# ScalarE and VectorE in program order through the feed-forward layers, their borders by token half, and products of a split grouped by engine

## The chip, the cores and the metric

One core of a Trainium2 chip runs the whole program. The metric is the device time of one execution in microseconds (us). A core has five engines that run their own queues in order: TensorE (PE, matrix products and transposes; PEld is its weight load), VectorE (DVE), ScalarE (ACT), GpSimd (POOL) and SyncE (SP), which here only issues transfers.

## The reference, cut to what matters

256 tokens of width 1024 pass through two stacked blocks in fp32. What the change touches are the five SwiGLU layers (width 2816) and what stands between them:

```python
def swiglu(h, w_gu, w_down):
    gu = h @ w_gu
    return (jax.nn.silu(gu[..., :D_FF]) * gu[..., D_FF:]) @ w_down
...
        x = x + rms_norm(y, g[1])
        y = memory_cross_attention(rms_norm(x, g[2]), mem_n, wq[i], wkv[i], wo[i])
        x = x + rms_norm(y, g[3])
        y = swiglu(rms_norm(x, g[4]), w_gu[i], w_down[i])
        x = x + rms_norm(y, g[5])
...
    for i in range(DEPTH_2):
        x = x + 0.5 * swiglu_2(rms_norm_2(x, ffn1_norm[i]), ffn1_w_gate[i], ffn1_w_up[i], ffn1_w_down[i])
        h = rms_norm_2(x, mix_norm[i])
        # i = 0: attention (8 heads, rotary, causal); i = 1: Mamba-2 (32 heads in 8 groups)
        x = x + 0.5 * swiglu_2(rms_norm_2(x, ffn2_norm[i]), ffn2_w_gate[i], ffn2_w_up[i], ffn2_w_down[i])
```

The first block normalizes each sublayer's output before it adds it to x (the gains g[1], g[3], g[5]); the second adds it as it is.

## The kernel before

Every weight comes in units of 128 x 2048 fp32 (1 MB). A unit is split into a high part, rounded to the matmul's fp32r type, and a low part, the rest. `unit` (L185) loads it into one of three raw buffers (SP), and for each of its two 1024-column halves ACT rounds it (L198 or L205, "cast") and DVE subtracts (L199 or L207, "rest"); for some units POOL subtracts. A product is then three matmuls: high by high, low by high, high by low (`mm`, L181). Activations are split likewise (`split`, L299). Cast halves live in four buffers each for high and low (`pw`); an "ahead" unit has two whole 1 MB tiles from a pool of seven that the normed input and x share (`p8`). There are four PSUM banks for passing use (`psb`) and four for sums (`psa`).

The order of PE's work is the order of the program (`manual_schedule` with PE alone, L930 and L937). The order of ACT's, DVE's, POOL's and SP's queues is chosen at build time by a scheduler that takes what is ready by its own estimate, earliest in the program first; `high_priority` moves instructions forward in that choice. `weave` (L463) interleaves PE's filling work (products with weights, a step at a time) with latency chains (heads, groups) that are due at given steps and name the steps until their next piece.

A feed-forward layer (`ffn`, L1079) has 11 chunks of 256 hidden columns. A chunk multiplies both token halves (128 tokens each) by two units of gate and up weights (`wide_step`, eight steps of six 512-column matmuls), evicts Silu(gate)*up (`evict`, L1094 on ACT, L1095 on DVE), and turns and splits the chunk before (`turned`, L1101, L301, L303) so that `down_steps` (L275) can multiply that by its down unit and add it up in the four sum banks. Chunks 0 and 10 go by token half. The last down unit alone goes by token half too, and after each quarter `Fin.done` (L410) updates x: where the output is normalized first, Square of the sums with a row sum (L426, ACT), the root (L430, L317 on DVE, L318 on POOL), scaling and adding (L436, L437, DVE) of both column halves; else one addition (L414). Then come the squares of x for the next norm (`PreT.square`, L370, ACT) and the turning of x into the next layer's input (`PreT.turn`: four transposes L378 on PE, then four scalings L383 on ACT and four rests L384 on DVE, in turn by column block). Where the output is normalized, all four turns are put off until after the last unit ("late"): two run before the next layer's first matmul and two after its steps 1 and 3.

The borders are: from the mixing stage to the memory attention (normalized, at 262 us of the profile; the last value unit `mem_v_unit` stands between, with two turns at its step 3 and two behind it), from there to the first layer (normalized, 333 us), to the second (normalized, 525 us), to the attention (720 us), back (840 us), to the fourth layer (1025 us), to the Mamba stage (1212 us), and to the last layer (1465 us).

The attention's chain of a head pair is `pair` (L1209): `rope_norm` (L1170), E0 = 5 steps, the turning of q and k (L1201), scores, E2 = 6 steps, the turning of the weights. `rope_tables` (L1027) are made behind the memory attention. The Mamba stage's chain is `group` (L1421): a convolution (L1402 DVE, L1405 ACT, taps L131 DVE), two pairs of heads whose decay sums PE multiplies out (two matmuls of `ahl` by `ohr`) and ACT evicts by four Relus (L1440), the two masked products of a head pair (L1452, DVE), D0 = 2 steps, the gate and turning, D1 = 5 steps, the output products (three banks), squares and root (L1496 to L1499), the root's product with a row scale (L1500, DVE), the scaling (L1502, ACT), D2 = 9 steps, and the turning of y. Every `wz` unit's rest is POOL's (L207 on POOL).

Of the kernel before, what the change touches and what calls it, by code (L numbers as in the profile page):

```python
# [97 lines left out]
def _build(ctx, nc, tc, a):  # L98
# [112 lines left out]

    def lin_step(bk, u, xh, xl, k, m, last=7):
# [7 lines left out]
    def lin_pair(bks, us, xh, xl, k, last=7):  # L220

        for lo_ in (False, True):
# [32 lines left out]
    def wide_step(bks, us, xh, xl, k, halves=(0, 1)):  # L255

        h, l = us[k // 4]
# [9 lines left out]
    def down_part(acc, u, hh, hl, th, o, k, first, last):  # L267
        t, c = slice(th * 128, th * 128 + 128), slice(o * 512, o * 512 + 512)
        h, l = u[0][k][:, c], u[1][k][:, c]
# [5 lines left out]
    def down_steps(acc, u, yf, first, fin=None, every=2):  # L275

        hh, hl = yf()
        if fin is not None:
            for th in range(2):
                for o in range(2):  # L280
                    for k in range(2):
                        down_part(acc, u, hh, hl, th, o, k, first, True)
                    fin.done(th, o)
                    yield
            return
# [77 lines left out]
    class PreT:  # L363
# [8 lines left out]
        def turn(self, xt, th, q):  # L372
# [8 lines left out]
            for i in range(4):  # L381
                k, b = 4 * q + i, bk[:, i * 128:i * 128 + 128]
                S.mul(self.xh[:, k, t], b, pc(gname, gi + k))  # L383
                V.scalar_tensor_tensor(self.xl[:, k, t], b, pc(gname, gi + k), f(self.xh[:, k, t]), MUL, SUB)  # L384
# [7 lines left out]
    class Fin:  # L392
# [10 lines left out]
        def turn(self, th, q):  # L403
            self.nxt.turn(self.xt, th, q)

        def turns(self, *w):
            for th, q in w:
                self.late.append(lambda th=th, q=q: self.turn(th, q))

        def done(self, th, o):  # L410
            xt, c = self.xt, slice(o * 512, o * 512 + 512)
            x, y = xt[:, th, c], flat(self.acc[2 * th + o])
            if self.post is None:
                V.tensor_tensor(x, x, y, ADD)  # L414
                if self.nxt is None:
                    nc.sync.dma_start(a["out"][:, th, c], x)
                    return
                self.nxt.square(th, o, x)
                if th:
                    self.turn(0, o)  # L420
                    self.turns((1, o))
# [9 lines left out]
            r = rstd(v, 1.0 / 1024, 1e-6, n=1)  # L431
            for o in range(2):
# [5 lines left out]
                self.nxt.square(th, o, x)  # L438
            self.turns((th, 0), (th, 1))
# [461 lines left out]
    def mem_v_unit(j, u, pool, late):  # L901
        mh_, ml_, rbm, rm = kv["x"]
        bk = bank(pool)
        for k in range(8):
            linT_step(bk, u, mh_, ml_, k)
            if k == 3:
                late.pop(0)()
# [6 lines left out]
    def wout_units():  # L914
        acc.extend([bank(psa), bank(psa), bank(psa), bank(psf)])
        for j, y in enumerate([y_r[0], *y_c]):
            hl = split(y)
            yield from down_steps(acc, unit(a["wout"][(2, 0, 1)[j]]), lambda: hl, j == 0, None, 1)
# [19 lines left out]
    order.__enter__()  # L938
    yl = split(y_r[1])
    u = unit(a["wout"][3])  # L940
# [4 lines left out]
    run(down_steps(acc, u, lambda: yl, False, fin))  # L945
    mem_v_unit(3, um, psb, fin.late)
    for t in fin.late:
        t()
# [3 lines left out]
    def two(n, l):  # L952
        return lambda: (unit(a[n][l * 22], True, ahead=True), unit(a[n][l * 22 + 1]))
# [54 lines left out]
    acc, nf = [], []  # L1008
    nxt2 = PreT("g4")
    fins = []  # L1010

    def outs_():
        acc.extend(new_acc())
        for h in range(4):
            u = unit(a["wo"][h], True)
            if h == 3:
                nf.extend(two("wgu", 0)())
                fins.append(Fin(xt, acc, nxt2, "g3r"))
            yield from down_steps(acc, u, lambda: oh[h], h == 0, fins[0] if h == 3 else None)

    fill = [first_heads()]
    for h in (2, 3):
        fill.append(pieces(lambda h=h: unit(a["wq"][h], True), qb[h]))
    fill.append(outs_())
    weave(fill, [(8, mem_head(0)), (9, mem_head(1)), (11, mem_head(2)), (15, mem_head(3))])

# [607 lines left out]
```

## Time and profile before

| what | value |
|---|---|
| median of the runs shown (3 runs) | 1662.89 us (1662.61 to 1665.56) |
| the profiled execution | 1663.16 us, span 1661.1 us |
| PE busy | 1600.0 us (96%) |
| DVE, ACT, POOL busy | 1058.9 (64%), 864.0 (52%), 142.9 us (9%) |
| mean granted TensorE clock | 0.987 |
| HBM read | 263.52 MB, 159 GB/s over the span |

The span runs from the first to the last instruction; 2.1 us lie around it. A matmul's shown length overlaps that of the next, so the rate is read from stretches, not from single lengths. The clock column of a stretch is the mean of the two levels that were granted, 1.00 (2.4 GHz) and 0.50 (1.2 GHz).

### The profile page before, as it was taken

The numbers are of one execution on the slowest core, as the hardware profiler recorded it, in microseconds if no ns is written. First come the engines' busy times: TensorE is split into PE (matmuls) and PEld (weight loads), VectorE is DVE, ScalarE is ACT, GpSimd is POOL, SyncE is SP. The second block draws the span as 40 slices with busy tenths as digits, with TensorE's granted clock in tenths as the row PEclk, the third lists the DMA queues.
The fourth block names the chain that finished last, engine by engine and source line by source line (L and its number), as shares of the span: only waits on it lengthen the run. The fifth ranks groups of instructions, "written<-read, shape, count | busy, mean of one in ns | idle before, by whom it ended". The sixth has DMA issues, their size and how long they took to land.

```text
span 1661.1 us, 21983 instructions
## 1 busy us (share of the span) xinstructions
PE 1600.0 (96%) x8702; PEld 1376.1 (83%) x8702; DVE 1058.9 (64%) x1652; ACT 864.0 (52%) x1432; POOL 142.9 (9%) x154
## 2 busy tenths in 40 slices
PE   8999998989999999999999999999999999999999
PEld 7898988878887888877778887888889889778887
DVE  6888855574545554567665556555559999665453
ACT  6734445563445444456664445444456766564442
POOL 2322200000000000000000000000014333000000
PEclk9999999989999999999999999999999999999999
DMA  7321234445454445452345554554533323455451
GB/s 280 133 76 53 88 131 149 150 147 213 165 217 157 159 181 200 172 193 92 140 191 200 179 193 175 188 201 170 195 121 129 151 102 127 150 206 194 186 188 66
DMA packets 39848, 265.99 MB, mean 160 GB/s; under 512 B 4673, under 2 KB 5441, under 8 KB 8385
## 3 DMA queue, kind: packets, MB, share of 16 engines
q1 hardware_dynamic: 39456, 263.41, 43.0%
q8 instruction: 68, 1.11, 0.3%
q10 hardware_dynamic: 288, 1.18, 0.2%
q14 instruction: 36, 0.29, 0.1%
HBM read 263.52 MB, written 1.05 MB: 159 GB/s over the span
## 4 chain that ended last, share of the span: by engine, by line
PE 77%; DVE 13%; ACT 6%; issue 3%; POOL 1%; DMA 0%; SPq 0%; POOLq 0%; ACTq 0%; DVEq 0%
PE bk L181 74%; DVE wl L207 3%; PE bk L1101 1%; ACT wh L205 1%; DVE s2w L1427 1%; DVE cv L131 1%; DVE s2w L131 1%; DVE sm L1500 1%; ACT s2w L1405 1%; ACT s2w L1440 1%; PE bk L740 1%; ACT s2n L370 0%; PE bk L378 0%; ACT s L383 0%; DVE s2w L436 0%
## 5 line engine op out<-in xcount | busy, mean ns | idle before, releaser
L181 PE MATMUL bk<-wh,s 128*128 128x512 f32 (+1 forms) x2400 | 735.6, 381 | 10.2 <-DVE s L384 4.8
L207 DVE TENSOR_TENSOR wl<-raw,wh 128x1024 fp32r<-128x1024 f32 x344 | 420.2, 1227 | 266.0 <-ACT wh L205 264.3
L205 ACT CAST wh<-raw 128x1024 fp32r<-128x1024 f32 x366 | 382.0, 1049 | 291.2 <-PE bk L181 278.9
L181 PEld LDWEIGHTS bk<-wh,s 128*128 128x128 f32 x2400 | 441.3, 190 | 94.4 <-DVE s L384 8.2
L181 PE MATMUL bk<-wl,s 128*128 128x512 f32 (+1 forms) x1200 | 449.8, 375 | 0.0
L181 PE MATMUL bk<-wh,s2f 128*128 128x512 f32 x1072 | 344.6, 392 | 0.0
L181 PEld LDWEIGHTS bk<-wl,s 128*128 128x128 f32 x1200 | 228.0, 190 | 37.0
L181 PEld LDWEIGHTS bk<-wh,s2f 128*128 128x128 f32 x1072 | 201.3, 188 | 41.6 <-issue 0.2
L181 PE MATMUL bk<-s,wh 128*128 128x256 f32 x1120 | 220.2, 296 | 8.7 <-ACT wh L528 5.9
L181 PE MATMUL bk<-wl,s2f 128*128 128x512 f32 x536 | 208.6, 389 | 0.0
L181 PEld LDWEIGHTS bk<-s,wh 128*128 128x128 f32 x1120 | 180.7, 197 | 12.8 <-ACT wh L528 5.9
L199 DVE TENSOR_TENSOR wl<-raw,wh 128x1024 fp32r<-128x1024 f32 x120 | 144.4, 1221 | 66.1 <-ACT wh L198 66.1
L181 PE MATMUL bk<-s,wl 128*128 128x256 f32 x560 | 160.3, 289 | 0.5 <-DVE wl L529 0.4
L198 ACT CAST wh<-raw 128x1024 fp32r<-128x1024 f32 x120 | 123.0, 1051 | 60.2 <-DMA raw<-f1gu 20.6
L303 DVE TENSOR_TENSOR s2f<-bk,s2f 128x512 fp32r<-128x512 f32 x59 | 40.8, 691 | 134.0 <-ACT s2f L301 133.9
L301 ACT CAST s2f<-bk 128x512 fp32r<-128x512 f32 x59 | 34.6, 586 | 171.2 <-PE bk L1101 168.9
L181 PEld LDWEIGHTS bk<-wl,s2f 128*128 128x128 f32 x536 | 100.7, 188 | 20.4
L181 PEld LDWEIGHTS bk<-s,wl 128*128 128x128 f32 x560 | 110.3, 197 | 1.3 <-DVE wl L529 0.9
L318 POOL TENSOR_TENSOR sm<-sm,mh 128x2 f32<-128x2 f32 (+1 forms) x17 | 17.1, 1003 | 775.0 <-DVE sm L317 346.8
L1094 ACT ACTIVATE s2w<-bk,sm 128x256 f32<-128x256 f32 x110 | 50.6, 472 | 36.2 <-PE bk L181 35.7
L1095 DVE SCALAR_TENSOR_TENSOR s2w<-bk,sm,s2w 128x256 f32<-128x256 f32 x110 | 51.9, 482 | 18.6 <-ACT s2w L1094 18.3
L207 POOL TENSOR_TENSOR wl<-raw,wh 128x1024 fp32r<-128x1024 f32 x22 | 54.9, 2499 | 68.3 <-ACT wh L205 68.2
(327 smaller groups left out, 1426.5 us busy)
## 6 DMA issues: line engine op xcount, KB each, us to landing
raw<-f1gu SPq DMA_DIRECT2D x44, 1024.0 KB, 4.8
raw<-f2gu SPq DMA_DIRECT2D x44, 1024.0 KB, 4.8
raw<-wgu SPq DMA_DIRECT2D x22, 1024.0 KB, 4.8
raw<-f1d SPq DMA_DIRECT2D x22, 1024.0 KB, 4.8
raw<-f2d SPq DMA_DIRECT2D x22, 1024.0 KB, 5.2
raw<-wxbc SPq DMA_DIRECT2D x16, 1024.0 KB, 4.8
raw<-wdn SPq DMA_DIRECT2D x11, 1024.0 KB, 6.4
raw<-win SPq DMA_DIRECT2D x10, 1024.0 KB, 4.8
```

The costliest lines, as they stand in the source:

```text
L131: V.scalar_tensor_tensor(o, src, w, o, MUL, ADD)
L181: PE.matmul(out, lhsT, rhs, start=start, stop=stop, skip_group_check=True)
L198: S.copy(h[:, c], r[:, c])
L199: V.tensor_tensor(l[:, c], r[:, c], f(h[:, c]), SUB)
L205: S.copy(h, r[:, c])
L207: (eng or V).tensor_tensor(l, r[:, c], f(h), SUB)
L301: S.copy(hh, src)
L303: V.tensor_tensor(hl, src, f(hh), SUB)
L318: G.tensor_tensor(r, r, mh[:, 0:n], POW)
L740: PE.transpose(bx[:, u], Z[:, u], ident)
L1094: S.activation(t, b[:, 0], AF.Silu, scale=r[:, th:th + 1])
L1095: V.scalar_tensor_tensor(t, b[:, 1], ru[:, th:th + 1], t, MUL, MUL)
```

## The change

Five edits. (1) `stretch` puts ACT and DVE in program order, as PE is, from the last two units of a mixer (or attention) through one or two feed-forward layers to their last border; the units' loads and casts are no longer issued at one place per unit but half a unit at a time by `feed()`, between PE's steps, under a plan (`Plan`) that allows four live cast halves and one ahead unit. (2) The last two down units, not one, go by token half (`down_two`); the turns of half 0 come inside the second half's work, the squares behind them, and the turns of half 1 after steps 1 and 3, or 5 and 7 where the output is normalized. (3) In a turn the four scalings come first, then the four rests. (4) The mixing stage's third output unit moves out of the weave into `down_two`, and the two late turns go to steps 6 and 7 of `mem_v_unit`; the rotary tables move into the memory attention's weave. (5) `rope_norm` runs at high priority, E0 = 7, E2 = 7, D1 = 6, D2 = 11, the weighing of the last two head pairs 4 steps later, and the product L1500 goes to POOL.

```diff
+    def feed():
+        if Plan.at == Plan.end:
+            return False
+        u = Plan.units[Plan.at]
+        if u.ahead and u.n == 0:
+            if Plan.ahead:
+                return False
+            Plan.ahead = 1
+        elif not u.ahead:
+            if Plan.live == 4:
+                return False
+            Plan.live += 1
+        load_more()
+        u.cast()
+        if u.n == 2:
+            Plan.at += 1
+            load_more()
+        return True
...
+    def load_more():
+        while Plan.loaded < min(Plan.end, Plan.at + 3):
+            Plan.units[Plan.loaded].load()
+            Plan.loaded += 1
...
+    def down_two(acc, u, yu, v, yv, fin):
+        for th in range(2):
+            hh, hl = yu(th)
+            for o in range(2):
+                if not th:
+                    feed()
+                for k in range(2):
+                    down_part(acc, u, hh, hl, th, o, k, False, False)
+            if th and fin.post is None:
+                fin.turn(0, 0)
+                fin.turn(0, 1)
+                feed()
+                fin.squares(0)
+            hh, hl = yv(th)
+            for o in range(2):
+                for k in range(2):
+                    down_part(acc, v, hh, hl, th, o, k, False, True)
+                fin.done(th, o)
+                if th and o == 0 and fin.post is not None:
+                    fin.turn(0, 0)
+                    fin.turn(0, 1)
+                    feed()
+                    fin.squares(0)
+        if fin.post is None:
+            feed()
+        fin.squares(1)
...
+            with tc.high_priority():
+                ks = [(4 * q + i, bk[:, i * 128:i * 128 + 128]) for i in range(4)]
+                for k, b in ks:
+                    S.mul(self.xh[:, k, t], b, pc(gname, gi + k))
+                for k, b in ks:
+                    V.scalar_tensor_tensor(self.xl[:, k, t], b, pc(gname, gi + k), f(self.xh[:, k, t]), MUL, SUB)
...
         def done(self, th, o):
+            with tc.high_priority():
+                self.update(th, o)
+            if th:
+                self.late.append(lambda: self.turn(1, o))
...
             r = rstd(v, 1.0 / 1024, 1e-6, n=1)
+            feed()
             for o in range(2):
...
+    IN_ORDER = {mybir.EngineType.Activation, mybir.EngineType.DVE}
+    def stretch(n, l, get, acc, nxt, post, layers, until):
+        u, v = unit(a[n][l - 2], True), unit(a[n][l - 1], True)
+        with tc.manual_schedule(engines=IN_ORDER):
+            u, v = started((u, v))
+            Plan.end = 1 + max(i for i, w in enumerate(Plan.units) if any(w is v for v in until))
+            fin = Fin(xt, acc, nxt, post)
+            down_two(acc, u, lambda th: get[l - 2], v, lambda th: get[l - 1], fin)
+            for units, nx, po in layers:
+                fin = ffn(units, fin.nxt, fin, nx and PreT(*nx), po)
+        return fin
...
     def ffn(units, pre, before, nxt, post=None):
+        late = dict(zip((1, 3) if before.post is None else (5, 7), before.late))
...
                     for k in range(8):
+                        feed()
                         wide_step(b, us, xh, xl, k, (th,))
+                        if c == 0 and th == 0 and k in late:
+                            late[k]()
+                        if c and th == 1 and k == 5:
+                            turned_last(0)
...
+            if 0 < c < 10:
+                for _ in down_steps(acc, dn[c - 1], lambda: hl, c == 1):
+                    feed()
         fin = Fin(xt, acc, nxt, post)
+        def last_but_one(th):
+            if th:
+                turned_last(1)
+            return hl
+        down_two(acc, dn[9], last_but_one, dn[10], lambda th: last, fin)
...
-    E0, E1, E2 = 5, 3, 6
+    E0, E1, E2 = 7, 3, 7
...
         G.tensor_tensor(rs, rs, mh[:, 0:2], POW)
-        V.tensor_tensor(rs, rs, rh, MUL)
+        G.tensor_tensor(rs, rs, rh, MUL)
...
-    D0, D1, D2 = 2, 5, 9
+    D0, D1, D2 = 2, 6, 11
```

The three `outs_` functions become one, `outs_of`, which leaves the last two units to `stretch`; `turned_last` turns and splits one token half of chunk 10.

## Rows read from the trace of the kernel before

**Rows 1.** The page, part 1: busy time of each engine over the span.
```profile
PE 1600.0 (96%) x8702; PEld 1376.1 (83%) x8702; DVE 1058.9 (64%) x1652; ACT 864.0 (52%) x1432; POOL 142.9 (9%) x154
```

**Rows 2.** The chain that ended last, two pieces (start us, us, what), first layer's inside.
```profile
364.32 16.37 PE bk L181 x72
381.12 16.37 PE bk L181 x72
```

**Rows 3.** Busy time by stretch: us, PE, PEld, DVE, ACT, POOL (x), PEclk, DMA, GB/s.
```profile
350.00:525.00 175.00, 175.00 (x794) 144.76 (x793) 94.53 (x118) 81.99 (x106) 1.54 (x1) 1.00 0.48 182
...
262.00:280.00 18.00, 12.80 (x82) 11.85 (x81) 11.62 (x30) 10.40 (x30) 1.25 (x2) 0.81 0.43 147
333.00:350.50 17.50, 13.25 (x47) 9.48 (x46) 12.95 (x35) 11.69 (x31) 1.08 (x2) 0.71 0.42 150
525.00:546.00 21.00, 16.49 (x66) 12.16 (x65) 16.64 (x34) 14.09 (x35) 1.08 (x2) 0.84 0.41 150
720.00:735.00 15.00, 14.20 (x70) 11.15 (x69) 12.26 (x24) 11.19 (x27) 1.70 (x1) 1.00 0.46 170
...
1212.00:1226.00 14.00, 12.89 (x76) 10.70 (x75) 11.08 (x24) 9.65 (x27) 0.42 (x4) 1.00 0.44 153
...
735.00:840.00 105.00, 99.31 (x474) 82.04 (x473) 71.47 (x149) 67.95 (x145) 6.54 (x4) 0.98 0.39 146
...
1300.00:1423.00 123.00, 110.47 (x857) 105.58 (x855) 112.87 (x197) 81.40 (x191) 38.70 (x32) 0.97 0.33 121
```

**Rows 4.** Timeline of PE at the border at 333 us: start, length, [idle before <-releaser].
```profile
337.93 1.32 PE L378 MATMUL bk<-idt,s 128*128 128x128 f32 x8 [1.17 <-DVE s L437]
340.81 0.80 PE L181 MATMUL bk<-wh,s 128*128 128x512 f32 x1 [1.56 <-ACT s L383]
...
344.98 0.80 PE L181 MATMUL bk<-wh,s 128*128 128x512 f32 x1 [1.49 <-DVE s L384]
```

**Rows 5.** PE's waits in the attention, 735 to 840: us, times, longest.
```profile
PE bk L1201 <- DVE s2w L1194: 5.6, 2, 4.0
```

**Rows 6.** PE's waits in the Mamba groups, 1300 to 1423: us, times, longest.
```profile
PE bk L181 <- ACT s2w L1440: 11.8, 7, 2.0
```

**Rows 7.** Groups of one chunk inside the first layer, 364.4 to 381.2: busy, mean ns.
```profile
L207 DVE TENSOR_TENSOR wl<-raw,wh 128x1024 fp32r<-128x1024 f32 x4 | 4.9, 1224 | 2.7 <-ACT wh L205 2.7
...
L205 ACT CAST wh<-raw 128x1024 fp32r<-128x1024 f32 x4 | 4.2, 1048 | 3.4 <-PE bk L181 3.4
```

**Rows 8.** ACT's waits over the span: us, times, longest.
```profile
ACT wh L198 <- DMA raw<-f2gu: 20.1, 15, 3.7
```

**Rows 9.** Timeline of DVE at the border at 333 us.
```profile
335.87 1.41 DVE L436 SCALAR_TENSOR_TENSOR s2w<-bk,sm,cv 128x512 f32<-128x512 f32 x2 [0.72 <-POOL sm L318]
337.19 1.28 DVE L437 TENSOR_TENSOR s<-s,s2w 128x512 f32<-128x512 f32 x2
338.39 2.35 DVE L207 TENSOR_TENSOR wl<-raw,wh 128x1024 fp32r<-128x1024 f32 x2
```

**Rows 10.** Timeline of ACT at the border at 333 us.
```profile
334.08 0.60 ACT L426 ACTIVATE s2n<-bk 128x512 f32<-128x512 f32 x1 [0.67 <-PE bk L181]
...
338.02 0.62 ACT L370 ACTIVATE s2n<-s 128x512 f32<-128x512 f32 x1
...
340.40 0.61 ACT L383 ACTIVATE s<-bk,pk 128x128 fp32r<-128x128 f32 x2
```

**Rows 11.** Two lines of the Mamba groups: count, duration ns min/median/max, first and last start.
```profile
L1500 DVE TENSOR_TENSOR sm<-sm,rh x8: 160/2352/2356, 1314.1 to 1437.3; 128x2 f32<-128x2 f32 x8
...
L1452 DVE TENSOR_TENSOR s2w<-s2w,s2o x16: 677/683/2474, 1293.9 to 1422.7; 128x512 f32<-128x512 f32 x16
```

**Rows 12.** Timeline of one Mamba group, 1336 to 1358 (all engines).
```profile
1341.43 0.50 PE L181 MATMUL bk<-ahl,ohr 128*128 128x256 f32 x2 [2.01 <-ACT s2w L1440]
...
1350.14 2.40 POOL L207 TENSOR_TENSOR wl<-raw,wh 128x1024 fp32r<-128x1024 f32 x1
1350.20 2.35 DVE L1500 TENSOR_TENSOR sm<-sm,rh 128x2 f32<-128x2 f32 x1 [0.49 <-POOL sm L1499]
```

More of the change, by code (lines that the diff above doesn't have):

```diff
@@ new lines, in feed, with need @@
+    def feed():
[16 more added lines that the diff above has]
+        return True
+    def need(u, i):
+        while isinstance(u, Unit) and u.n <= i:
+            assert feed()
@@ L212, in lin_step, with done @@
+    def done(u, i):
+        if isinstance(u, Unit) and i not in u.dead:
+            u.dead.add(i)
+            if not u.ahead:
+                Plan.live -= 1
+            elif len(u.dead) == 2:
+                Plan.ahead = 0
     def lin_step(bk, u, xh, xl, k, m, last=7):
@@ L403, in turn, with squares, update @@
         def turn(self, th, q):
[L404 to L408, printed above, removed]
-        def done(self, th, o):
+            if self.nxt is not None:
+                self.nxt.turn(self.xt, th, q)
+        def squares(self, th):
+            if self.nxt is not None:
+                for o in range(2):
+                    self.nxt.square(th, o, self.xt[:, th, o * 512:o * 512 + 512])
+        def done(self, th, o):
+            with tc.high_priority():
+                self.update(th, o)
+            if th:
+                self.late.append(lambda: self.turn(1, o))
+        def update(self, th, o):
             xt, c = self.xt, slice(o * 512, o * 512 + 512)
@@ L1006, in mem_head @@
         oh[h] = split(bk)
[L1008 to L1025, printed above, removed]
+    acc = []
+    rope = {}
     def rope_tables():
@@ L1087, in ffn @@
         ts = {}
-        pend = None
+        last = []
+        gu, dn = units
         def evict(c, b, th):
@@ L1102, in turned, with turned_last @@
             return split(bk, "f")
+        def turned_last(th):
+            if not last:
+                last.extend((s2("f", F32R), s2("f", F32R)))
+            bk, t = bank(), slice(th * 128, th * 128 + 128)
+            for i in range(2):
+                PE.transpose(bk[:, i, 0:128], ts[10][:, th, i * 128:i * 128 + 128], ident)
+            split(bk[:, :, 0:128], "f", last[0][:, :, t], last[1][:, :, t])
+        hl = None
         for c in range(11):
-            us = nf if c == 0 else (unit(a[wgu][l * 22 + 2 * c], True, ahead=True), unit(a[wgu][l * 22 + 2 * c + 1], True))
+            us = gu[c]
             b = bank(), bank()
@@ L1263, in _build @@
     ao = [None] * 4
[L1264 to L1276 removed]
+    acc = []
+    fill = [wide(lambda: uqk, qk[0], late_, True)]
     for j in range(1, 4):
@@ L1297, in _build @@
     V.tensor_copy(ohr, C("oneh"))
-    for t in late:
+    for t in fin.late:
         t()
```

237 lines of the change are left out of this document (123 added, 114 removed).

## The prediction

> **What bounds the kernel now.** I read the page's busy shares first: PE is busy for 96% of the span [rows 1]. Whether that is its full rate is seen in the chain that ended last: inside a feed-forward layer it is PE alone, 72 matmuls in 16.37 us, 0.227 us each, a chunk every 16.81 us [rows 2]. The stretches agree: from 350 to 525 us PE has no idle time, ACT is busy for 82 and DVE for 94.5 of 175 us [rows 3]. The change removes no matmul, so inside the five layers it can only lose. What it can win lies between them: window less PE's busy time, plus what the lower clock costs. At the three normalized borders PE is idle for 5.2, 4.25 and 4.5 us, and the mean clock is 0.81, 0.71 and 0.84 [rows 3]. With levels of 1.00 and 0.50 that is 6.8, 10.2 and 6.7 us at 1.2 GHz; half of the part in which PE works is lost. Taking 1, 2.5 and 1.7 us of it as idle, the loss is 2.9, 3.8 and 2.5 us. So these borders cost 8.1, 8.1 and 7.0 us. The second shows how: PE's first turns wait for DVE's update of x, its first matmuls for ACT's scaling, then for DVE's rests [rows 4]. The plain border at 720 us idles 0.8 us at full clock; those at 840, 1025 and 1465 us look the same; that at 1212 us idles 1.1 us [rows 3]. The attention idles 5.7 us, 5.6 of them at the turning of rotated heads, with some 4 us at half clock [rows 3, 5]. The Mamba groups idle 12.5 us, 11.8 of them in seven waits for ACT's Relus, the longest 2.0 us [rows 3, 6]; there DVE is busy for 112.9 of 123 us, so DVE nearly bounds that stage. All this comes to about 50 us of 1661.
>
> **Inside the layers: nothing.** ACT and DVE in program order put every cast before whatever follows it in the program, so a late weight would hold up the evictions. A step of a chunk is six matmuls, 1.36 us, and a chunk has 12 places to feed for its six half-unit casts of 1.05 us on ACT and 1.22 us on DVE [rows 2, 7]. By the plan's limits an ahead half is cast at steps 4 and 5 for the next chunk's steps 0 and 2, eight steps or 10.9 us early, and the other halves 9 to 12 steps early, against 2.3 us for a cast and its rest. The queues run 7.8 and 9.0 us of work per 16.8 us. The transfers keep three raw buffers and still wait for a freed one; ACT waits up to 3.7 us for one now [rows 8], inside that lead. I count 0; the bounds are 0 and the rival below.
>
> **Normalized borders.** Before, the update of token half 0 was covered by half of the last unit, 12 matmuls or 2.7 us; with two units by half it is 24, 5.4 us. From the Square of the last sums to DVE's scaling it is 335.87 - 334.08 = 1.8 us, then 0.70 and 0.64 us per column half [rows 9, 10]: x is there after 3.1 and 4.5 us. The first turn now stands 18 matmuls (4.1 us) behind, so half 0 no longer stalls PE. At 262 us ACT and DVE stay with the scheduler, the update at high priority. Its half 1 is covered by 7 and 8 steps of a value unit, six 256-column products each (0.68 us at half of 0.227, an estimate): 4.8 and 5.5 us against 3.1 and 4.5. I keep 1 us of stalls: **-7.1 us** (bounds 0 and -8.1).
>
> At 333 and 525 us program order costs something. In the second half ACT has, ahead of the Square of the last sums: eight scalings (0.61 per two, 2.4), one cast (1.05) and two squares of x (0.62 plus a read, 1.5) [rows 7, 10]. They start about 4.9 us after half 0 ended and finish at 9.8, while PE ends half 1 at 24 x 0.227 + 0.9 for 8 transposes (1.32 with a stall in it [rows 4]) = 6.4 us. Then the new `feed` in the update puts a cast and its rest (1.05 + 1.22) ahead of DVE's scaling: x of half 1 at 14.2 us. PE asks for it after five to six steps of half a chunk (18 matmuls), at 10.5: a wait of 3.8 us, and 0.9 more at its own half 1, where ACT still has the squares to do. With 1.7 us for a lower clock that is 6.4 each, against 8.1 and 7.0: **-2.3 us** together (bounds: -15.1 if the last Square isn't held up, +3 if half 0 stalls too).
>
> **Plain borders.** One addition per quarter, and turns of half 0 under 12 more matmuls: the four idle times of 0.8 us go, **-3.2 us** (bounds 0 and -4). At 1212 us both halves of the next matmul need half 1's turn; I count 0 (bounds -1.1 and +2, where ACT's cast and squares, 1.05 + 1.5 us, stand ahead of the scalings). Scalings grouped by engine save the alternation, inside these terms. The rotary tables leave the second border, where their small DVE operations stood between the rests; under the memory attention they have idle DVE time. 0 beyond the above.
>
> **Attention.** E0 gives two steps, 2.7 us, and high priority takes `rope_norm` past casts' rests of 1.22 us on DVE [rows 7]. The longest wait is 4.0 us [rows 5]; 2.7 + 1.22 about covers it, and the clock loss behind it goes. **-6.5 us** (bounds 0 and -7.2). What waits behind: casts, with more than a unit of lead. The chain now ends one step before the last two units; split and turning of the last pairs are due 2.7 and 4.1 us ahead of use, so 0 to +1.5 us, kept for the range.
>
> **Mamba groups.** DVE's product L1500, on two numbers per partition, takes 2352 ns in the median and 160 at least [rows 11]: it starts 0.06 us behind POOL's 2.40 us rest and ends with it [rows 12]. On POOL, in order behind the root, that is 2.2 us of DVE's time back in each group. POOL's own product is a like operation to the root, which DVE awaits for 0.72 us [rows 9]; POOL has time (38.7 of 123 us). It can delay the scaling of y, which D2 covers with two more steps. About 0.6 us I take back, since POOL's rest now ends later and DVE's next cast rest may meet it. 1.6 x 7 = **-11 us**; bounds 0 (below) and -15 (all idle time and clock loss). D1 moves three banks' use a step later, so that the Relus have a step more; the next user of a bank there is the group's score product, hidden if DVE's gain reaches ACT.
>
> The sum: -7.1 - 2.3 - 3.2 - 6.5 - 11 = -30.1. From the profiled execution, 1663.16 us (2.1 of it outside the span): 1633.1; the median of the runs stands 0.3 below it: **1633 us**, 1.8% less.
>
> **Rivals.** (a) The lock passes on. Behind L1500 DVE has L1452, whose operands also both lie in SBUF; it took 2474 ns once against 683 [rows 11]. If it meets POOL's rest in each group, nothing is won there: 1644. For it: that one row, and POOL's rest stands right behind. Against: L1452 is ready while POOL still works on the root, before the rest. The Trainium skill (SBUF — State Buffer, Who interferes with whom) has it that a DVE instruction with two SBUF inputs and a GpSimd one that reads SBUF shut each other out for a whole instruction. By that rule the product's move frees nothing unless L1452 starts first, and the time would be the 1644 of this rival; the trace agrees on the lock (L1500 ends with POOL's instruction) and doesn't show who goes first. Chance 0.16.
>
> (b) The normalized borders come out clear, the last Square not held up: 13 us less, 1620. For it: the update is written at high priority, and a scheduler that honours that within program order puts the last Square first. Against: the order written in the program. Chance 0.20.
>
> (c) Slower: program order at ACT. A load that lands later than its cast's place holds the Silu behind it. It decides from the point where a cast is later than its lead of 8 steps, 10.9 us; then every chunk pays. ACT now waits 1.3 us a time for `f2gu` [rows 8]; at that price 10 chunks of 5 layers lose 65 us: 1698. Against: the lead, and PE's 175 us without idle time under the same three buffers. Chance 0.09.
>
> (d) No change: what is won at the borders is given back at the next one, since PE sets the rate of all else; 1662. The idle windows speak against it. Chance 0.03.
>
> **How the numbers follow.** My forecast of 1633 has 0.52. A measurement of this kernel can tell 0.2% (3.3 us) from no change. Faster: 0.52 + 0.16 + 0.20 = 0.88; same 0.03; slower 0.09. The low end, 1612, is the sum with nearly all of the 50 us gone; the high end, 1653, is (a) with the attention's and half of the first border's gain missing too. Outside lie (c), (d) and a little of either tail, 0.2 in all.
>
> **What would show it.** Right: 16.8 us per chunk and no PE idle time inside layers; at 262 us under 1.5 us idle and no low clock; L1500's place on POOL, L1452 at 0.68 us and PE's waits for the Relus under 1 us; no 4 us wait at L1201. At 333 and 525 us I expect one wait of 3 to 4 us for half 1's update, with ACT's squares of half 0 ahead of the last Square. Wrong: PE waiting for casts or evictions inside a layer, L1452 at 2.4 us, new waits for banks in the groups, or PE waiting at the attention's end for the last split.

## The result, and the profile after

The changed kernel takes 1649.34 us (median of four runs, 1647.85 to 1650.24) against 1662.97 us before: a ratio of 0.9915 [0.9902, 0.9927], 13.6 us less where 30 were forecast. The profiled execution took 1650.06 us with a span of 1648.2 us; before it was 1663.16 and 1661.1.

Part 1 of the changed kernel's page answers [rows 1]:

```profile
PE 1594.3 (97%) x8702; PEld 1374.2 (83%) x8702; DVE 1051.7 (64%) x1649; ACT 859.5 (52%) x1437; POOL 147.1 (9%) x162
```

Where the time went is read from marks: the time at which the chain that ended last reaches the same matmul, found by its place in PE's order, in both traces. How far the distance between two marks grew (+) or shrank (-) is what the stretch between them lost or gained.

| stretch up to the mark, by the times of before | mark before (us) | mark after (us) | change (us) | forecast (us) |
|---|---|---|---|---|
| mixing stage, unchanged | 229.71 | 230.73 | +1.0 | 0 |
| borders at 262 and 333 | 364.32 | 358.25 | -7.1 | -8.8 |
| border at 525 | 559.28 | 552.48 | -0.7 | -0.6 |
| border at 720, attention, border at 840 | 862.65 | 851.93 | -3.9 | -8.1 |
| border at 1025 | 1050.74 | 1039.54 | -0.5 | -0.8 |
| border at 1212 | 1237.32 | 1229.05 | +2.9 | 0 |
| Mamba groups, border at 1465 | 1489.04 | 1476.15 | -4.6 | -11.8 |
| last layer | 1661.1 | 1648.2 | 0.0 | 0 |

So three stretches hold what is missing: the attention, the border at 1212, and above all the Mamba groups. The busy time by stretch, answering [rows 3]; the columns are us, then PE, PEld, DVE, ACT and POOL busy, the granted clock, DMA share and GB/s:

```profile
262.00:280.00 18.00, 15.17 (x115) 14.99 (x114) 12.63 (x34) 11.40 (x28) 1.26 (x2) 0.91 0.59 206
331.00:348.50 17.50, 14.77 (x66) 11.80 (x65) 12.18 (x29) 11.21 (x31) 0.55 (x1) 0.90 0.25 91
...
1203.00:1217.00 14.00, 11.23 (x60) 9.46 (x59) 9.73 (x24) 10.46 (x28) 0.42 (x4) 0.88 0.40 151
...
1290.00:1412.00 122.00, 112.34 (x870) 107.63 (x869) 104.28 (x196) 82.08 (x191) 47.10 (x41) 0.97 0.34 122
```

At 262 us PE works 2.4 us more of 18 and the clock is 0.91, not 0.81; the border at 1212 is the one that got worse, 11.2 of 14 us busy at 0.88, against 12.9 at 1.00. In the groups DVE is busy for 104 of 122 us, down from 113 of 123: it has back the time that the forecast gave it, yet PE still idles for 9.7 us, at a clock of 0.97. PE's waits over the whole span say for what (us, times, longest):

```profile
PE bk L491 <- DVE s L556: 8.3, 4, 2.8
PE bk L181 <- ACT s2w L1579: 6.8, 6, 2.3
...
PE bk L491 <- DVE s L537: 4.5, 5, 2.0
...
PE bk L181 <- ACT s2c L1356: 2.0, 1, 2.0
...
PE bk L181 <- DVE s2f L416: 1.6, 1, 1.6
```

L556 is the update of x at the normalized borders (L437 before), L537 the addition at the plain ones, L1579 the Relus (L1440 before), L1356 the copy of a turned q or k, L416 the split of turned hidden columns. Inside the layers next to nothing changed, as forecast: PE waits twice there, 0.4 and 0.5 us for a cast's rest at 352 and 546 us, right behind the normalized borders. The chain that ended last has the same piece as [rows 2], the 72 matmuls of a chunk:

```profile
358.25 16.37 PE bk L181 x72
```

**The border at 1212.** The timeline of ACT, DVE and PE's turns at that border in the changed kernel (start, length, what, [idle before <- releaser]):

```profile
1206.61 2.16 DVE L499 SCALAR_TENSOR_TENSOR s<-bk,pk,s 128x128 fp32r<-128x128 f32 x8 [3.52 <-ACT s L497]
...
1208.68 1.22 DVE L233 TENSOR_TENSOR wl<-raw,wh 128x1024 fp32r<-128x1024 f32 x1
...
1209.82 1.28 DVE L537 TENSOR_TENSOR s<-s,bk 128x512 f32<-128x512 f32 x2
...
1210.55 1.25 PE L491 MATMUL bk<-idt,s 128*128 128x128 f32 x8 [1.99 <-DVE s L537]
1210.56 1.10 ACT L205 CAST wh<-raw 128x1024 fp32r<-128x1024 f32 x1
...
1211.51 0.67 ACT L483 ACTIVATE s2n<-s 128x512 f32<-128x512 f32 x1
...
1212.13 2.21 ACT L497 ACTIVATE s<-bk,pk 128x128 fp32r<-128x128 f32 x8
```

DVE's additions for half 1 (L537) stand behind the eight rests of half 0's turn (L499) and the rest of a fed cast (L233); ACT's scalings (L497) stand behind a cast and a square. PE waits 2.0 us for the one and 0.8 us for the other, and part of the stretch runs at the lower level (0.88 in the mean).

**A normalized border.** At 333 us the order of the program shows in the same way. PE ended half 1's sums near 335.4 us; the Square of them (L544, on ACT) begins at 337.65, behind a cast and two squares of half 0, and the scaling (L555, on DVE) stands behind one more rest:

```profile
337.65 0.65 ACT L544 ACTIVATE s2n<-bk 128x512 f32<-128x512 f32 x1
```

```profile
339.36 1.23 DVE L233 TENSOR_TENSOR wl<-raw,wh 128x1024 fp32r<-128x1024 f32 x1 [0.59 <-ACT wh L232]
340.50 0.74 DVE L555 SCALAR_TENSOR_TENSOR s2w<-bk,sm,cv 128x512 f32<-128x512 f32 x1
```

This is the wait that the prediction described: PE idles 2.4 us here and 2.7 us at the border at 525, where it said 3.8.

### The profile page after: what moved, and what is told of

It reads as the page before. It is cut to its first block, busy times and chain, and to the rows that moved or that the text cites. A ratio compares the mean times of both kernels' runs of the same rounds, so it can differ in the third digit from the quotient of the medians.

```text
span 1648.2 us, 22085 instructions
## 1 busy us (share of the span) xinstructions
PE 1594.3 (97%) x8702; PEld 1374.2 (83%) x8702; DVE 1051.7 (64%) x1649; ACT 859.5 (52%) x1437; POOL 147.1 (9%) x162
## 4 chain that ended last, share of the span: by engine, by line
PE 79%; DVE 10%; ACT 6%; issue 3%; POOL 1%; DMA 0%; SPq 0%; POOLq 0%; DVEq 0%; ACTq 0%
PE bk L181 76%; DVE wl L207 2%; PE bk L1239 1%; DVE cv L131 1%; ACT s L497 1%; ACT s2w L1579 1%; ACT wh L205 1%; DVE s L499 1%; PE bk L491 1%; PE bk L857 1%; DVE wl L233 1%; ACT wh L232 1%; ACT s2n L483 0%; POOL sm L431 0%; DVE s2n L1541 0%
## 5 line engine op out<-in xcount | busy, mean ns | idle before, releaser
L233 DVE TENSOR_TENSOR wl<-raw,wh 128x1024 fp32r<-128x1024 f32 x338 | 403.9, 1223 | 156.4 <-ACT wh L232 156.3
L232 ACT CAST wh<-raw 128x1024 fp32r<-128x1024 f32 x338 | 348.5, 1052 | 147.0 <-PE bk L181 146.6
L205 ACT CAST wh<-raw 128x1024 fp32r<-128x1024 f32 x142 | 147.7, 1052 | 68.8 <-PE bk L181 57.1
L207 DVE TENSOR_TENSOR wl<-raw,wh 128x1024 fp32r<-128x1024 f32 x120 | 147.7, 1241 | 54.2 <-ACT wh L205 53.9
L416 DVE TENSOR_TENSOR s2f<-bk,s2f 128x512 fp32r<-128x512 f32 (+1 forms) x64 | 41.6, 650 | 208.6 <-ACT s2f L414 208.5
L414 ACT CAST s2f<-bk 128x512 fp32r<-128x512 f32 (+1 forms) x64 | 35.4, 553 | 257.5 <-PE bk L1239 225.2
L431 POOL TENSOR_TENSOR sm<-sm,mh 128x2 f32<-128x2 f32 (+1 forms) x17 | 13.1, 769 | 786.2 <-DVE sm L430 786.2
```

The costliest lines, as they stand in the source:

```text
L205: S.copy(h, r[:, c])
L207: (eng or V).tensor_tensor(l, r[:, c], f(h), SUB)
L232: S.copy(h, self.raw[:, c])
L233: self.eng.tensor_tensor(l, self.raw[:, c], f(h), SUB)
L414: S.copy(hh, src)
L416: V.tensor_tensor(hl, src, f(hh), SUB)
```

## Experiments

All ratios are to the kernel before, timed on the same chip. Every profile was also read by the marks above, stretch by stretch: the unchanged mixing stage alone differs by up to 2.1 us between profiles, which a total takes in and a mark behind it does not.

### The Mamba groups

Two edits met there: the product went to GpSimd, and D1 and D2 grew. First each was undone.

```diff
# e2_groups_as_before
-        G.tensor_tensor(rs, rs, rh, MUL)
+        V.tensor_tensor(rs, rs, rh, MUL)
-    D0, D1, D2 = 2, 6, 11
+    D0, D1, D2 = 2, 5, 9
# e3_product_on_dve: the first pair of lines alone
# e4_steps_as_before: the second pair of lines alone
```

> The changed kernel with the Mamba groups as before: the root's product on VectorE, D1 = 5 and D2 = 9. Theory: the groups' edit gave about 4 us, so 1653, and PE's seven waits of 2.0 us for the Relus are back at the decay sums' second matmul; DVE is busy for about 112 of the 122 us. Rival, the working of the prediction (DVE's time is PE's time there): 11 us, 1660.

> The changed kernel with the root's product back on VectorE alone, D1 = 6 and D2 = 11 kept. Theory, bank rotation: PE waits for a PSUM bank that ACT's Relus free, and DVE has time to spare, so the product's place is worth little: 0 to 1.5 us, 1649 to 1651, although DVE is busy for some 10 us more of the groups' 121. Rival, DVE's time sets the pace: 7 to 11 us slower, 1656 to 1660.

> The changed kernel with D1 = 5 and D2 = 9 and the root's product on GpSimd. Theory, bank rotation: the output products take three banks between the two pairs' decay sums again, so the second pair's matmul waits for the first pair's Relus in each group, 2.0 us each: 3 to 4 us slower than the changed kernel, 1652 to 1653, with DVE's busy time as low as in the changed kernel. Rival, DVE's time sets the pace: the waits shrink without the new step counts, 1649.

Measured: e2 1652.95 us, 0.9940 [0.9925, 0.9955]; e3 1649.99 us, 0.9922 [0.9906, 0.9939]; e4 **1639.50 us**, 0.9861 [0.9843, 0.9879]. The first two came at the expected times. The third went the other way from its theory: the old step counts with the product on GpSimd are 10 us faster than the changed kernel. Its rival had the waits shrink, as they did, but not the size. So with the old counts the product's move is worth a lot, and the new counts spend it.

e3 hit its time for another reason than it gave. It expected DVE to be busy for some 10 us more in the groups; DVE is busy for 104.1 of 122 us there, as in the changed kernel. With the new counts the product no longer meets GpSimd's rest, though it stands on VectorE (duration in ns, min/median/max):

```profile
L1639 DVE TENSOR_TENSOR sm<-sm,rh x8: 160/161/565, 1307.6 to 1426.9; 128x2 f32<-128x2 f32 x8
```

In e2, with the old counts, the same line took 2348 ns in the median. So both edits take away the same lock, each by itself, and the new counts bring a loss of their own. The direct test of the line alone is the kernel before with it:

```diff
-        V.tensor_tensor(rs, rs, rh, MUL)
+        G.tensor_tensor(rs, rs, rh, MUL)
```

> The kernel before with one line of the change: the root's product of the Mamba groups on GpSimd (L1500). The prediction's term for it was 11 us (bounds 0 and 15). Theory: that term was right, and what spent it in the changed kernel were the new step counts; so 1651 to 1653, PE's waits for the Relus at the decay sums' second matmul fall from seven of 2 us to under 0.5 us each after the first groups, and the groups take 16 us each. Rival: the gain in the kernel with D1 = 5 and D2 = 9 came from elsewhere in the change (program order at the border before, other casts): 1658 to 1663.

Measured: 1648.64 us, 0.9918 [0.9903, 0.9933], 14.3 us less, more than its theory had; one line brings as much as the whole change. The window of the groups of this kernel, its waits of PE there, the product, and ACT's scaling of y behind the product, before and in this kernel:

```profile
1300.70:1408.50 107.80, 106.01 (x855) 102.44 (x854) 96.98 (x190) 80.50 (x189) 37.91 (x36) 1.00 0.39 138
```

```profile
PE bk L1507 <- ACT s2w L1440: 1.2, 1, 1.2
PE bk L181 <- ACT s2w L1440: 0.4, 1, 0.4
```

```profile
L1500 POOL TENSOR_TENSOR sm<-sm,rh x8: 194/194/195, 1313.3 to 1422.8; 128x2 f32<-128x2 f32 x8
```

```profile
1352.65 0.91 ACT L1502 ACTIVATE s2f<-s2f,sm 128x256 f32<-128x256 f32 x2 [2.73 <-DVE sm L1500]
```

```profile
1345.51 0.91 ACT L1502 ACTIVATE s2f<-s2f,sm 128x256 f32<-128x256 f32 x2 [0.56 <-POOL sm L1500]
```

Seven waits of up to 2.0 us [rows 6] have become two, of 0.4 and 1.2 us, the clock is 1.00, and a product that took 2352 ns beside GpSimd's rest [rows 11] takes 194 ns. The way from the product to PE leads over ACT: before, ACT stood still for 2.73 us until the product was there, and the Relus that PE waits for come later in ACT's queue; now it stands still for 0.56 us. L1452 stays at 682 ns in the median, so the lock did not pass on to it. The Trainium skill (SBUF — State Buffer, Who interferes with whom) has the rule that a VectorE instruction with two SBUF inputs and a GpSimd one that reads SBUF exclude each other. The trace agrees, and shows two ways out: the small product stands on GpSimd's own queue, ahead of the long rest (e13), or it starts on VectorE just before the rest does (e3).

What the step counts do was asked one count at a time:

```diff
# e9_five_eleven               # e10_six_nine                # e7_three_steps
-    D0, D1, D2 = 2, 6, 11
+    D0, D1, D2 = 2, 5, 11     # = 2, 6, 9                   # = 2, 7, 10
```

> The changed kernel with D1 = 5 alone, D2 = 11 kept, the root's product on GpSimd. Theory, bank rotation: D1 decides, because with 5 steps the three output banks are taken between the two pairs' decay sums, so that the two pairs' Relus come due 4 us apart; with 6 steps both pairs' Relus come due within the same 4 us. So the groups take 16 us each as in the kernel with D1 = 5 and D2 = 9, about 10 us less than the changed kernel: 1638 to 1641. Rival, D2 decides (the later turning of y holds a bank or the queue of ACT): no gain, 1649.

> The changed kernel with D2 = 9 alone, D1 = 6 kept. Theory, bank rotation: D1 decides, so PE still waits for the second pair's Relus at the score matmul, about 1.2 us in each group: 1648 to 1651. Rival, D2 decides: 1638 to 1641.

> The changed kernel with D1 = 7 and D2 = 10. Theory, bank rotation: the output products' banks are then taken behind the score product, two and three steps behind the decay sums whose Relus free them, so PE waits for Relus under 0.5 us: about 8 to 11 us less than the changed kernel, 1638 to 1642. Rival, as the kernel with D1 = 6 and D2 = 9 showed: the next holder in the rotation decides, here the turning of y or of x, whose bank waits for VectorE's sums; then 1648 or more.

Measured: e9 1644.43 us, 0.9892 [0.9877, 0.9908]; e10 1660.18 us, 0.9988 [0.9979, 0.9998]; e7 1645.54 us, 0.9899 [0.9882, 0.9915]. The table gives the length from the first decay sum to the same matmul of the last layer (its border included), in us:

| product on | D1, D2 | length |
|---|---|---|
| VectorE (kernel before) | 5, 9 | 203.1 |
| GpSimd (e13, in the kernel before) | 5, 9 | 190.6 |
| VectorE (e2) | 5, 9 | 203.7 |
| VectorE (e3) | 6, 11 | 200.6 |
| GpSimd (e4) | 5, 9 | **188.9** |
| GpSimd (e9) | 5, 11 | 195.5 |
| GpSimd (changed kernel) | 6, 11 | 198.5 |
| GpSimd (e7) | 7, 10 | 197.9 |
| GpSimd (e10) | 6, 9 | 211.3 |

Kernels with the changed kernel's groups (e1, e5, e6, e8, e11) took 198.9 to 200.8 us here, so differences of 2 us say little: 7 and 10 is not better than 6 and 11. With the product on VectorE the new counts gain 3.1 us, for they also take the lock away; with it on GpSimd, where the lock is gone already, they lose 9.6. The two counts don't add up: D1 = 5 for 6 brings 3.0 us at D2 = 11 and 22.4 at D2 = 9; D2 = 9 for 11 brings 6.6 at D1 = 5 and costs 12.8 at D1 = 6. The theory that D1 alone decides holds in sign; e9 and e10 both missed their times. In e10 PE waits for something else, the turning of y (L1646), and VectorE's L1566 and L1636 take long beside GpSimd's rest (L1636 took 154 ns in the median in the changed kernel). PE's waits of e10, one of them in the timeline, and L1636:

```profile
PE bk L1646 <- DVE s2f L1629: 9.6, 5, 1.9
```

```profile
1373.60 2.37 POOL L207 TENSOR_TENSOR wl<-raw,wh 128x1024 fp32r<-128x1024 f32 x1 [8.73 <-ACT wh L205]
...
1374.09 2.44 DVE L1566 SCALAR_TENSOR_TENSOR s2w<-s2n,s2w 128x512 f32<-128x512 f32 x1 [1.84 <-ACT s2n L1565]
...
1376.92 1.03 PE L1646 MATMUL bk<-idt,s2f 128*128 128x128 f32 x4 [1.92 <-DVE s2f L1629]
```

```profile
L1636 DVE TENSOR_TENSOR sm<-sm,rq x8: 154/1928/1942, 1303.6 to 1435.3; 128x2 f32<-128x2 f32 x8
```

VectorE's sum L1629, for which PE waits, stands behind the long L1566. e4 has the long L1566 too, but behind that sum.

Why the counts cost time in the changed kernel is seen by setting one of its groups beside one of e4. PE takes four banks for passing use in turn. In the changed kernel both decay sums (`ahl`) come before the output products (`s2w`, then `s1v`), and the score product (`s,s`) waits:

```profile
1384.42 0.40 PE L181 MATMUL bk<-ahl,ohr 128*128 128x256 f32 x2
...
1386.09 1.95 PE L181 MATMUL bk<-s2w 128*128 128x128 f32 x16
1387.88 0.60 PE L181 MATMUL bk<-s1v,s2o 128*128 128x256 f32 x2
1389.41 0.81 PE L181 MATMUL bk<-s,s 128*128 128x256 f32 x3 [0.94 <-ACT s2w L1579]
```

The second pair's decay sums are written at 1384.42 and their bank is wanted again 4 us later. In that time ACT's queue has this to do, the first pair's Relus included:

```profile
1385.23 1.12 ACT L1579 ACTIVATE s2w<-bk,acT 128x128 f32<-128x128 f32 x4
1386.23 1.05 ACT L205 CAST wh<-raw 128x1024 fp32r<-128x1024 f32 x1
1387.16 0.64 ACT L1580 ACTIVATE s2w<-s2w 128x512 f32<-128x512 f32 x1
1387.69 0.37 ACT L1579 ACTIVATE s2w<-bk,acT 128x128 f32<-128x128 f32 x1
1387.94 0.64 ACT L1565 ACTIVATE s2n<-s2w 128x512 f32<-128x512 f32 x1
1388.46 0.90 ACT L1579 ACTIVATE s2w<-bk,acT 128x128 f32<-128x128 f32 x3
```

In e4 the output products stand between the two pairs, so the second pair's decay sums come just as the first pair's Relus end (1373.75 on ACT), and the score product waits for nothing:

```profile
1371.38 1.95 PE L181 MATMUL bk<-s2w 128*128 128x128 f32 x16
1373.17 0.60 PE L181 MATMUL bk<-s1v,s2o 128*128 128x256 f32 x2
1373.80 0.50 PE L181 MATMUL bk<-ahl,ohr 128*128 128x256 f32 x2
...
1376.01 0.71 PE L181 MATMUL bk<-s,s 128*128 128x256 f32 x3
```

So the new counts let the Relus of both pairs fall due within one 4 us stretch instead of two. That the bank is what PE waits for is inferred from the order in which the program takes the banks; the trace names only the Relus. e7 fits it: with D1 = 7 the waits at the score product are gone, and PE waits up to 1.15 us in five groups at the last output product (`s1v`). That is the fourth product to take a bank behind the second pair's decay sums there, as the score product is in the changed kernel. The profile names no releaser for these waits, but each ends 0.1 us behind the second pair's last Relu, which ended at 1369.16 us in this group:

```profile
1369.25 0.67 PE L181 MATMUL bk<-s1v,s2o 128*128 128x256 f32 x2 [1.14 <-issue]
```

So e7 moved the wait and did not remove it; its time lies between theory and rival. The Trainium skill (Perfetto Trace Analysis, Matmuls) advises to rotate matmuls through banks so that one's eviction overlaps the next. The rows agree, and add that the order of the takers counts: with the same four banks the stretch took 188.9 us in e4 and 198.5 us in the changed kernel.

### The borders

```diff
# e1_squares_behind: at every border
                 fin.turn(0, 1)
-                feed()
-                fin.squares(0)
...
+        feed()
+        feed()
+        fin.squares(0)
         fin.squares(1)
# and in half 1's normalized update no feed()
# e11_updates_first: normalized: the feed() behind the turn stays; plain: squares(0) stays,
#                    then the additions, squares(1), feed(), feed()
```

> The changed kernel with the fed casts and the squares of half 0 put behind the updates of half 1 at every border, and without the cast inside half 1's normalized update. Theory, queue order: at 333 us ACT's Square of half 1's last sums began 2.2 us after PE had ended them, behind a cast and the two squares, and DVE's scaling stood 1.0 us behind a cast's rest; with that gone PE's waits of 2.4 and 2.7 us at 339 and 533 us go, and the half clock behind them: 3 to 4 us each. The four waits of 0.8 us at the plain borders go too, and 2 of the 3 us that the border to the Mamba stage lost. At 262 us, where ACT and DVE are not in program order, 0 to 3 us. In all 10 to 14 us less than the changed kernel, about 1637. Rival, the update's own latency: from the last Square to x are 3.1 and 4.5 us whatever stands ahead, and the cover is too short; then waits of over 2 us stay and the time is 1647 or more. Second rival: casts that come later are missed by the first chunks, new waits for casts, 1650 or more.

> The changed kernel with another order at the borders: where the output is normalized, the cast behind half 0's turn stays, but the squares of half 0 and the cast inside half 1's update go behind that update; at the plain borders the squares of half 0 stay and the casts go behind half 1's additions and squares. Theory, queue order within what the casts allow: the weights' casts were due there too, so a normalized border gains about 1.2 us at 339 and 533 us and not the whole 2.6 and 2.9; the waits of 0.8 us at 722, 834, 1022 and 1459 us go, and 2 us at 1208. 6 to 9 us less than the changed kernel, 1640 to 1643. Rival, ACT and DVE are full at a normalized border whatever the order: nothing is won there, and the casts put back cost something, 1644 to 1650.

Measured: e1 1651.82 us, 0.9933 [0.9919, 0.9948]; e11 1656.18 us, 0.9963 [0.9949, 0.9977]; both slower than the changed kernel. For e1 it is the second rival; e11 is slower still than its rival had it. In e1 the update at the border at 333 is on time but for 0.3 us, and PE waits for the weight instead. PE's waits of e1 from 331 to 345 us, then the longest of e11 from 715 to 735, a plain border where casts had been put back:

```profile
PE bk L181 <- DVE wl L233: 3.3, 1, 3.3
```

```profile
PE bk L181 <- ACT wh L232: 2.8, 1, 2.8
```

At these places the casts were due where they stood: each of the two orders only changed what came late. By the marks e1 does gain at the plain borders: 0.9 us at 722, 0.8 at 1022 and 1459, and 2.2 us at 1208, so there the order was the loss. e1 lost 2.8 us again at the border at 262, 2.2 us at 533, and 4.4 us where the attention's first pair waits for its rotated heads, whose norm needs the squares that now came late.

If these orders don't serve at the normalized borders, does the free one?

```diff
# e8_free_order
-        with tc.manual_schedule(engines=IN_ORDER):
+        if True:
```

> The changed kernel with ACT and DVE left to the scheduler's choice in the feed-forward layers and their borders, the plan of loads, the two units by half and the rest of the change kept. Theory: inside the layers PE sets the pace either way, 16.37 us for 72 matmuls; at the borders the order differs by 1 to 3 us each way, so 1645 to 1655. Rival: the program order is what holds the borders and the layers together; without it casts come late and the time goes back to 1660 or more.

Measured: **1636.06 us**, 0.9837 [0.9823, 0.9852], 13 us less than the changed kernel and outside both ranges. By the marks, 3.2 us came back at 333, 5.3 at 525 and 4.2 at 1212, and 1.3 was lost in the attention. PE's waits of this kernel at the three borders (326 to 345, 512 to 545, 1190 to 1210 us), in this order:

```profile
PE bk L491 <- DVE s L556: 1.1, 1, 1.1
```

```profile
PE bk L491 <- DVE s L556: 1.1, 1, 1.1
```

```profile
PE bk L491 <- DVE s L537: 0.5, 1, 0.5
```

The changed kernel's are 2.7 us in two waits at the first, 2.7 and 1.6 (L416) at the second, 2.0 and 0.8 at the third. The scheduler puts the last split (L416) into the 0.7 us in which DVE waits for the root, where program order has it behind the whole update. At 1212 it puts two casts ahead of half 0's scalings, not between them and the additions. Inside a layer the free order is as good as the other, with no idle PE:

```profile
343.00:510.00 167.00, 167.00 (x757) 138.10 (x757) 89.66 (x98) 76.19 (x93) 1.61 (x1) 1.00 0.54 195
```

### The attention

```diff
# e6_copy_first                          # e5_rope_free: rope_norm without
-        S.copy(qF, bk)                  #   tc.high_priority()
+        with tc.high_priority():
+            S.copy(qF, bk)
```

> The changed kernel with ACT's copies of the turned q and k at high priority as well. Theory: in the attention PE's wait of 2.0 us at 767.6 us is for the copy of k, which stood on ACT behind eight scalings of the next pair that the high priority had put ahead and that themselves waited for DVE and GpSimd; ahead of them, the wait goes to under 0.5 us: 1.5 to 2 us less between 740 and 820 us, nothing elsewhere, 1647 to 1648. Rival: the scheduler's estimate puts the copy behind them again, since it expects the scalings to be ready first: no change.

> The changed kernel with the rotation and its norm (rope_norm) left at the scheduler's choice, E0 = 7 and E2 = 7 kept. Theory: the two more steps of E0 alone, 2.7 us, take the waits for the rotated heads from 4.0 and 1.6 us to about 1.3 and 0; the high priority gave the other 1.2 us and cost the wait of 2.0 us for the copy of k: so the attention comes out within 1 us of the changed kernel, 1648 to 1650. Rival, the high priority carried the whole of it: waits of 3 to 4 us are back, 1652 or more.

Measured: e6 1646.46 us, 0.9904 [0.9886, 0.9922]; e5 1646.91 us, 0.9901 [0.9884, 0.9917]; both end up to 1.1 us under the ranges of their theories. By the marks e6 gains 2.3 us in the attention, the wait for the copy is gone, and nothing else moves there; e5 comes out 0.3 us ahead of the changed kernel. Without the high priority no wait for rotated heads (L1354) is left in e5, so the two more steps of E0 took the long waits by themselves. The high priority brought nothing that these runs show: with it 1.3 us of a wait for heads is left (at 749 us) and 2.0 us for the copy of k; without it one wait of 1.4 us for such a copy, at a later pair. The timeline of ACT and PE at the copy, in the changed kernel:

```profile
766.50 2.18 ACT L1341 ACTIVATE s2w<-bk,sm 128x128 f32<-128x128 f32 x8 [1.09 <-DVE sm L1335]
...
769.20 0.63 ACT L1356 COPY s2c<-bk 128x512 f32<-128x512 f32 x1
...
769.89 0.92 PE L181 MATMUL bk<-s2c 128*128 128x128 f32 x4 [1.99 <-ACT s2c L1356]
```

The eight scalings of the next pair (L1341) stand ahead of the copy and themselves waited 1.1 us.

### Put together

```diff
# e12_all_three: e4 + e6, and e1's order at the plain borders except the one into the attention
# e14_free_and_steps: e4 + e6 + e8
```

> The changed kernel with three edits: D1 = 5 and D2 = 9 (about 10.6 us in the groups), the copies of the turned q and k at high priority (2 us), and, at the plain borders except the one into the attention, the casts and the squares of half 0 behind half 1's additions (0.8 us at 834, 1022 and 1459 us, 2.2 us at 1208). The three lie in stretches of their own, so the sum should hold: 16 to 17 us less than the changed kernel, 1632 to 1634. Rival: what is won at one place is given back at the next, as in the kernel with all updates first: 1638 or more.

> The changed kernel with ACT and DVE left to the scheduler in the layers and at their borders, D1 = 5 and D2 = 9, and the copies of the turned q and k at high priority. Theory: the three losses lie in stretches of their own and add up: 13 us for the program order, 9.8 for the step counts, 3 for the copy (its wait was 3.0 us under the free order), so 1623 to 1626. Rival: the scheduler orders the queues anew over the whole program, and part of the 13 us is lost elsewhere: 1628 or more.

Measured: e12 1631.31 us, 0.9809 [0.9794, 0.9824]; e14 **1623.43 us**, 0.9759 [0.9745, 0.9774], 40 us less than before and 26 less than the changed kernel. Both sums held, the first a little exceeded: 18 us less than the changed kernel where 16 to 17 were expected, and 1623 us where 1623 to 1626 were. In e14 PE is busy for 1586.2 of 1622.1 us, and the largest of its waits behind the mixing stage is:

```profile
PE bk L491 <- DVE s L556: 5.0, 3, 2.8
```

Of these 5.0 us 2.8 are the border at 262, which no run here mended: it is outside `stretch`, and in e1 and e11 the wait only passed on to the next eviction.

## Why the prediction was right and wrong

- **Direction and range** held; the size didn't, 13.6 us for 30. The places to win were named rightly, PE's waits at the borders and in the groups, and the interior cost 0.9 us where 0 was counted. Rival (c) is out: the only waits for a cast inside the layers are these two. Rival (d) is out too. (By [rows 2] a chunk takes 16.80 us and not 16.81; nothing hangs on it.)
- **Mamba groups, -11, measured -4.6 with the border at 1465.** The term for the product was right as a mechanism and a little low: alone it measured 12.5 us of the groups and the border behind them (203.1 to 190.6), though before the product was locked in six groups of the eight and not in seven. Rival (a) is out as it was put, L1591 (L1452 before) took 684 ns in the median; but e10 shows that a change of counts can pass the lock on to another operation. The step that failed is "D1 moves three banks' use a step later, so that the Relus have a step more; the next user of a bank there is the group's score product, hidden if DVE's gain reaches ACT". It was put at nothing, and D1 and D2 cost 9.6 us together (e4 against the changed kernel). DVE's busy time in the groups fell by 8.6 us, but PE waits for the moment at which ACT's Relus end, and with the new counts both pairs' Relus fall due together. One of the text's own signs of being wrong, new waits for banks in the groups, is what came. The text also took the two edits as independent: by e3 the new counts take the lock away without the move, so the move's gain is not there twice.
- **Border at 1212, 0 with an upper bound of +2, measured +2.9.** The bound named ACT's cast and squares ahead of the scalings, which cost 0.8 us; the larger wait, 2.0 us, is for DVE's additions behind the rests, and the lower clock comes with it. The step that failed is the 0: the order of DVE's queue there was not counted. e1 took 2.2 us of it back by order alone.
- **Attention and its two borders, -8.1, measured -3.9.** The wait of 4.0 us went, by E0's two steps (e5). "What waits behind: casts, with more than a unit of lead" was the step that failed: the copy of k waits behind too, 2.0 us, and 1.3 us of the first pair's wait stayed. e6 gives 2.3 back. At the two plain borders 0.6 us of waiting stayed each.
- **Plain borders, -0.8 each, measured -0.5 at 1025.** Waits of 0.3 us for ACT's scaling and 0.5 us for DVE's rest went, and one of 0.6 us for DVE's addition came, behind the fed cast's rest. Most of the waiting went from one place to another; e1, without that rest ahead, gains 0.8 us there.
- **Normalized borders, -7.1 and -2.3, measured -7.1 for 262 and 333 together and -0.7 at 525.** The wait and its cause came as described, at 2.4 and 2.7 us and not 3.8. The nine other runs with the same code at 262 and 333 show -6.3 to -8.6 there, so the -8.8 was near. What the text did not see is that at 525 the last split waits behind the update (1.6 us), and that the border at 262, without program order, has the same wait (2.8 us, where the text kept 1 us): there the scheduler put two casts and the squares ahead of the last Square in spite of its high priority (it begins at 265.4 us, where PE had ended the sums near 262).
- **Rival (b), 13 us more from clear borders**, did not come: the waits of 2.4 and 2.7 us are there. That e8, without the program order, gains 13 us is the same number by chance: 8.5 of them lie at 333 and 525, 4.2 at 1212.

## What to carry to other kernels

Two edits that take away the same bottleneck do not add up: the new counts gained 3.1 us where the lock was still there, by taking it away, and cost 9.6 where the other edit had already done so. So measure the parts of a change one by one, the one-line part alone included; here it was worth the whole. And when step counts change, look at each short operation of the stretch for a new lock or a new wait, not at the old one alone. Writing an engine's order by hand needs every due time: at the normalized borders, with casts, updates and turns on two engines, each fixed order tried here made something late, and leaving the order to the scheduler was 13 us better over the whole program.

## What the hardware showed that was not expected

The clock behind a wait is not the same from profile to profile. At the border at 333 us the changed kernel and e3 run the same code around the same wait of PE, 2.4 us idle behind the same update. In the changed kernel's profile the clock then falls to the lower level for a while (0.90 over the stretch, above); in e3's it does not fall:

```profile
330.30:347.80 17.50, 14.37 (x69) 11.10 (x69) 12.28 (x30) 11.29 (x32) 1.25 (x2) 1.00 0.24 91
```

By the marks that is 1.1 us, and e4 shows 1.00 there too. The changed kernel's own four executions have mean clocks of 0.991 to 0.994. So part of the loss that was counted behind each wait differs between profiles of the same code, and a stretch of one profile is known to about a microsecond.
